# Second layer's compression MLP half a gate later, a fixed order of preparation, and A's attention in one group for each row tile

## The chip, the cores and the metric

One core of one Trainium2 chip runs the whole program. The metric is device time in microseconds (us), the median of several executions; one execution was taken with the hardware profiler, and its trace is what the rows below are from. Engines: PE is TensorE's matmul side, DVE is VectorE, ACT is ScalarE, POOL is GpSimd, SP is SyncE, whose queue issues the DMAs.

## The reference

Two layers of a decoder trunk on x of 256 tokens by 1024. In each layer h = RMSNorm(x), and one projection h @ w_in feeds four token mixers and four merge gates:

```
A  sparse attention: an indexer scores all keys, the best 64 of each query are attended to
   (4 query heads, one shared key/value head that comes from a latent of 128)
B  block attention, causal over all 256 keys (4 heads)
C  NSA: compressed blocks of 32 tokens (an MLP: gelu(z @ w1) @ w2), selected blocks, a window
D  sliding window of 128 with sinks (2 key/value heads)
br    = mixer output (256 wide) @ w_branch[n]             for each of the four
x     = x + (sum over n of sigmoid(gate[n]) * br[n]) @ w_out
x     = x + ConvFFN(RMSNorm(x))                           up, depthwise conv, SiLU product, down
```

Queries and keys of each mixer are normed per head and rotated first. That is the mixer's preparation.

## The kernel before

The program is written by a planner. Every piece of work is a Python generator that yields the engine, the values it needs and the buffer rings it takes from; `Flow.run` keeps a clock for each engine, always lets on the generator that can start earliest (then by priority), and so fixes the order of each engine's instructions when the program is built. On the chip each engine then runs its own list in order and waits where data are late.

Weights come in chunks of up to 1 MB in the order of the list `plan`, through a ring of three `raw` buffers on SP's queue. Each chunk is split in pieces of 128 x 1024 into a high part (`hi`, on ACT) and a low part (`lo`, on DVE), four buffers each. A product takes three matmuls: high by high, high by the low part of the activations, low by high. A raw buffer comes free when its last `lo` is done. An exception is the first weight of the compression MLP (`hidden`), which is used as it lands: its raw buffer comes free when its matmuls are done.

The generator `main` writes the large matmuls in a fixed order. First the projection columns, mixer by mixer in the order A, C, B, D. Then comes the list `SEQ`: gates in halves of 512 columns, the two MLP products for the keys and values of C (`hidden`, 64 matmuls on 32-row tiles in all), and the branch products. Mixer work goes in between wherever the planner finds it ready. TensorE's list is one queue: what stands behind a `hidden` that waits, waits too.

A mixer's preparation works in one shared set of buffers (`prep_r`, a ring of one): a mixer takes it, squares and sums its heads, takes a reciprocal root on POOL, rotates, transposes, and gives it back. The order in which the four get it is whatever the planner comes to. Preparation of C ends in the MLP's input `z` (the sums `kr<-kn,col`), for which `hidden` waits.

The attention of a mixer is `attend2`: scores of both row tiles (128 queries each) in one visit, for which two banks of the ring `mm_r` and both of `sc_r` are taken, then a softmax for each tile, then the value products of both tiles in one visit (`values`). Scores run on 64-row tiles of the array, value products on 64-column tiles, everything else on the whole array. A's `attend2` needs the selection masks of both tiles, `sel[0]` and `sel[1]`, which DVE finds in eight rounds of maximum and replace for each tile.

In the trace all instructions of a helper carry line L214, so tile names tell them apart: `mm<-hi,ahi` is a gate or projection product, `mm<-raw,kr` the MLP, `tr<-cst,f` a transpose, `mm<-qk` and `sc<-qk` scores, `tr<-f,kvA` A's value products.

Of the kernel before, what the change touches and what calls it, by code (L numbers as in the profile page):

```python
# [12 lines left out]
ALU = mybir.AluOpType  # L13
# [218 lines left out]
def trunk(ctx: ExitStack, tc: tile.TileContext, a, out):  # L232
# [151 lines left out]
    def rows_chunk(src, k0, k1, c0, c1):  # L384
# [7 lines left out]
        if not plan:  # L392
# [1 line left out]
        plan.append(Chunk(ap, (nk, n), cut))  # L394


    SEQ = [("gate", 0, 0), ("gate", 0, 1), ("hidden", 0, 0), ("hidden", 1, 0), ("gate", 1, 0),
           ("gate", 1, 1), ("branch", 0, 0), ("branch", 0, 1), ("gate", 2, 0), ("gate", 2, 1),
           ("branch", 1, 0), ("branch", 1, 1), ("gate", 3, 0), ("branch", 2, 0), ("branch", 2, 1),
           ("branch", 3, 0), ("gate", 3, 1), ("branch", 3, 1)]  # L400
    FIRST, LAST = [n for op, n, _ in SEQ if op == "branch"][0], SEQ[-1][1]
    PRIO = (4, 19, 7, 6)
    PORDER = (0, 2, 1, 3)
    CH_A, CH_C = [(0, 384), (384, 680)], [(1448, 1832), (1832, 2100)]
# [4 lines left out]
    for l in range(DEPTH):  # L409
        wi = a["w_in"][l]  # L410
        for kg in range(2):
            for _, c0, c1 in COLS[:2]:
                rows_chunk(wi, 4 * kg, 4 * kg + 4, c0, c1)
        for _, c0, c1 in COLS[2:]:
            for kg in range(2):
                rows_chunk(wi, 4 * kg, 4 * kg + 4, c0, c1)
        for op, n, half in SEQ:
            if op == "gate":
                for kg in range(2):
                    c0 = 2612 + n * D + half * 512  # L420
                    rows_chunk(wi, 4 * kg, 4 * kg + 4, c0, c0 + 512)
            elif op == "hidden":
                ap = a["c_cmp_w1"][l, n].rearrange("(c p) h -> p c h", p=128)
                plan.append(Chunk(ap, (16, 128), []))
            elif n == LAST:
                rows_chunk(a["w_branch"][l, n], 0, 2, half * 512, half * 512 + 512)
            elif half == 0:
                ap = a["w_branch"][l, n].rearrange("(k p) n -> p k n", p=128)
                plan.append(Chunk(ap, (2, D), [lambda v, h=h: v[:, :, h * 512:h * 512 + 512] for h in range(2)]))
        for kg in range(2):  # L430
            for half in range(2):
                rows_chunk(a["w_out"][l], 4 * kg, 4 * kg + 4, half * 512, half * 512 + 512)
        up = a["w_up"][l].rearrange("(k p) (g n) -> p k g n", p=128, g=2)
        for c in range(0, KF, 2):
            for g in range(2):
                plan.append(Chunk(up[:, :, g, c * 128:c * 128 + 256], (8, 256),
                                  [lambda v, h=h: v[:, :, h * 128:h * 128 + 128] for h in range(2)]))
        for half in range(2):
            for k0, k1 in DOWN:
                rows_chunk(a["w_down"][l], k0, k1, half * 512, half * 512 + 512)  # L440
# [188 lines left out]
    def T_pairs(o, src, n, needs):  # L629
# [8 lines left out]
        tr_r.give(tb, te)  # L638
        return te

    def attend2(prio, qT, kblk, kT, vfn, scl, masks, y, needs, sink=None, fin=None, gates=None):

        got = yield "PE", needs, [sx_r, sm_r, sx_r, sm_r, mm_r, mm_r, sc_r, sc_r]
        P.side = 2
        for t in range(NT):
            nk = 128 * (t + 1)

            for hh in range(2):
                for par in range(2):
                    b = 64 * par  # L650
                    te = P.matmul(got[4 + 2 * t + par][:, hh * nk:hh * nk + nk], qT[b:b + 64, hh, t * 128:t * 128 + 128],
                                  kT[b:b + 64, kblk(2 * hh + par), :nk], start=True, stop=True)
        P.side = 1
        pts, evs = [None, None], [[Fut() for _ in range(t + 1)] for t in range(NT)]
        for t in range(NT):
            fl.spawn(softmax(t, got[2 * t], got[2 * t + 1], got[4 + 2 * t:6 + 2 * t], (mm_r, sc_r)[t], te, scl, masks[t], sink,
                             None if gates is None else gates[t], pts, evs[t]), prio + t)
        yield from values(vfn, pts, evs, y, gates is not None, fin)
# [140 lines left out]

    def dsa(l, pa, pf, y, yf):  # L800
        m = M[l]
        (prep,) = yield "ACT", [pf, col_f[l]], [prep_r]
        rt, qr, kr, kn = prep
        latT = kn[:, :, 128:256]
        tl = yield from head_rstd(pa[:, :, None, 256:384], 1, 128, sm1["rl"], rt, [])
# [34 lines left out]
        for t in range(NT):  # L840
# [12 lines left out]
        tq = yield from T_pairs(qT, qr, 2, [tq])  # L853
        tk = yield from T_pairs(kT, krd, 1, [tk])
        prep_r.give(prep, tk)
        fin = qk_done(qk, [], yf, 1)
        fl.spawn(attend2(10, qT, lambda h: 0, kT, lambda h, b: kvA[:, b, 64:128], th(sm1["sA"], H), sel,
                        y, [tq, tk] + self_f, fin=fin), 10)

    def indexer(t, iqT, ikT, iw, needs, fin, f):  # L860
        nk = 128 * (t + 1)
# [32 lines left out]
        f.t = V.tensor_tensor(sel[t], sel[t], mask, op=ALU.min)  # L894

    def moba(l, pb, pf, y, yf):
        (prep,) = yield "ACT", [pf, tab_f[l]], [prep_r]
        rt, qr, kr, kn = prep
        tr = yield from head_rstd(heads(pb[:, :, 0:512]), 8, DH, sm1["rB"], rt, [])
        yield from scaled(sm1["sB"], sm1["rB"], 8, tr)  # L900
        tq = yield from rope(qr.rearrange("p t (h u d) -> p t h u d", u=1, d=64), heads(pb[:, :, 0:256]), H, DH,
                             cc[:, 2], ss_[:, 2], rt, [])
        (qk,) = yield "PE", [], [qk_r]
        qT, kT = qk[:, 0:512].rearrange("p (k s) -> p k s", k=2), qk[:, 512:1024].rearrange("p (k s) -> p k s", k=2)
        tq = yield from T_pairs(qT, qr, 2, [tq])
        yield "DVE", [], []
        tn = V.tensor_tensor(heads(kn), heads(pb[:, :, 256:512]),
                        th(sm1["rB"], 8)[:, :, 4:8, None].to_broadcast([128, NT, H, DH]), op=ALU.mult)
        tk = yield from rope(kr.rearrange("p t (h u d) -> p t h u d", u=1, d=64), heads(kn), H, DH, cc[:, 3], ss_[:, 3], rt, [tn])
        tk = yield from T_pairs(kT, kr, 2, [tk])  # L910
        prep_r.give(prep, tk)
        fin = qk_done(qk, [], yf, 1)
        fl.spawn(attend2(20, qT, lambda h: h // 2, kT, lambda h, b: pb[:, b, 512 + 64 * h:576 + 64 * h],
                        th(sm1["sB"], H), [tri[:, 128:], tri], y, [tq, tk], fin=fin), 20)

    def swa(l, pd, pf, y, yf):
        (prep,) = yield "ACT", [pf, tab_f[l]], [prep_r]
        rt, qr, kr, kn = prep
        tr = yield from head_rstd(heads(pd[:, :, 0:384]), 6, DH, sm1["rD"], rt, [])
        yield from scaled(sm1["sD"], sm1["rD"], 6, tr)  # L920
        tq = yield from rope(qr.rearrange("p t (h u d) -> p t h u d", u=1, d=64), heads(pd[:, :, 0:256]), H, DH,
                             cc[:, 8], ss_[:, 8], rt, [])
        (qk,) = yield "PE", [], [qk_r]
        qT, kT = qk[:, 0:512].rearrange("p (k s) -> p k s", k=2), qk[:, 512:1024].rearrange("p (k s) -> p k s", k=2)
        tq = yield from T_pairs(qT, qr, 2, [tq])
        yield "DVE", [], []
        knv = heads(kn[:, :, 0:128])
        tn = V.tensor_tensor(knv, heads(pd[:, :, 256:384]),
                        th(sm1["rD"], 6)[:, :, 4:6, None].to_broadcast([128, NT, 2, DH]), op=ALU.mult)
        tk = yield from rope(kr.rearrange("p t (h u d) -> p t h u d", h=2, d=64), knv, 2, DH, cc[:, 9], ss_[:, 9], rt, [tn], dup=2)  # L930
        tk = yield from T_pairs(kT, kr, 2, [tk])
        prep_r.give(prep, tk)
        fin = qk_done(qk, [], yf, 1)
        fl.spawn(attend2(30, qT, lambda h: h // 2, kT,
                        lambda h, b: pd[:, b, 384 + 64 * (h // 2):448 + 64 * (h // 2)], th(sm1["sD"], H),
                        [tri[:, 128:], dmask], y, [tq, tk], sink=M[l]["sink"], fin=fin), 30)

    def nsa(l, pc, pf, y, yf, hid):
        m = M[l]
        (prep,) = yield "DVE", [pf, tab_f[l]], [prep_r]  # L940
        rt, qr, kr, kn = prep
        kvd = kr.rearrange("p t (i u d) -> p t i u d", i=2, u=2)
        t1 = yield from rope(kvd[:, :, 0:1], pc[:, :, None, 256:320], 1, DH, cosd, sind, rt, [], dup=2)
# [322 lines left out]
    def main():  # L1266
# [13 lines left out]
        for l in range(DEPTH):  # L1280
# [11 lines left out]
            proj = (pa, pb, pc, pd)  # L1292
            ys = [p[:, :, 0:256] for p in proj]
            yf = [Fut() for _ in range(4)]
            def mixer(n, f):
                if n == 2:
                    fl.spawn(nsa(l, pc, f, ys[2], yf[2], hid), PRIO[2])
                else:
                    fl.spawn((dsa, moba, None, swa)[n](l, proj[n], f, ys[n], yf[n]), PRIO[n])
# [65 lines left out]
                        k0 = 4 * half + 2 * j  # L1365
                        fl.spawn(rows_T(mg[:, :, 128 * k0:128 * k0 + 256], [f], mT, k0, mf[2 * half + j], scale=0.5), 2)

            order = [n for op, n, half in SEQ if op == "branch" and half == 0]
            for i, n in enumerate(order):
                yTs[n] = [], Fut()  # L1370
                fl.spawn(y_T(ys[n], yf[n], *yTs[n]), 2)
            for op, n, half in SEQ:
                if op == "gate":
                    yield from gate_of(n, half)
                elif op == "hidden":
                    yield from hidden(n, next(it), hid)
                else:
                    yield from branch_out(n, half)
# [108 lines left out]
```

## Time and profile before

| | |
|---|---|
| median of 3 runs | 851.69 us (851.65 to 853.23) |
| the profiled execution | 850.18 us, span 848.4 us |
| PE busy | 835.4 us, 98% of the span |
| DVE, ACT, POOL busy | 673.0, 543.8, 36.5 us |
| mean granted TensorE clock | 0.994 |
| DMA | 149.91 MB, mean 177 GB/s |

The span is from the first to the last instruction. A busy PE is not PE at its peak: matmuls are pipelined and their ends are modelled, so the step from one start to the next tells more than a duration.

### The profile page before, as it was taken

The page shows a single profiled execution, that of the slowest core. Times are in us where ns is not written, and L with a number is a line of the kernel's source. Part 1 is how long each engine was busy: PE and PEld are TensorE (multiplying, and loading weights), DVE is VectorE, ACT ScalarE, POOL GpSimd, SP SyncE. Part 2 cuts the span into 40 slices and gives each one's busy share as a digit, 9 for nine tenths or more (in the row PEclk, how much of TensorE's full clock was granted, in tenths as well). Part 3 has the DMA queues.
Part 4 walks back from the last instruction along what each step waited for, and adds up shares of the span by engine and source line. Part 5 has one row for each costly group of instructions (what it writes and reads, how often), then busy time and mean ns, then how long its engine had stood idle before and what let it go on. Part 6 is the DMA issues. An engine that isn't in the chain of part 4 may idle for free.

```text
span 848.4 us, 14190 instructions
## 1 busy us (share of the span) xinstructions
PE 835.4 (98%) x5459; PEld 733.1 (86%) x5459; DVE 673.0 (79%) x1327; ACT 543.8 (64%) x941; POOL 36.5 (4%) x33
## 2 busy tenths in 40 slices
PE   9999999999999999999999997999999999999998
PEld 8987787888899999978898875878878999999886
DVE  5799989788579999975458989977676799999552
ACT  6673775765478888844366667766445788888431
POOL 0111111000000000000001110100000000000000
PEclk9999999999999999999999997999999999999999
DMA  7754563444647666546456453435455465665550
GB/s 264 248 199 149 178 216 106 159 162 153 219 138 229 207 201 197 186 153 210 132 168 211 157 173 115 148 117 182 162 192 192 149 199 199 200 199 199 175 197 26
DMA packets 103414, 149.91 MB, mean 177 GB/s; under 512 B 4072, under 2 KB 62258, under 8 KB 103346
## 3 DMA queue, kind: packets, MB, share of 16 engines
q1 hardware_dynamic: 103346, 149.00, 52.6%
q8 instruction: 43, 0.70, 0.3%
q14 instruction: 25, 0.20, 0.1%
HBM read 147.94 MB, written 1.05 MB: 176 GB/s over the span
## 4 chain that ended last, share of the span: by engine, by line
PE 86%; DVE 7%; DMA 2%; POOL 2%; ACT 1%; issue 1%; SPq 0%; DVEq 0%; ACTq 0%
PE mm L214 75%; PE tr L214 6%; PE sc L214 5%; DVE lo L214 2%; DMA raw<-in_w_in_dram 1%; POOL rB L214 1%; DVE acc L214 1%; DVE rt L214 1%; DMA x<-in_x_dram 1%; POOL rD L214 1%; DVE m L214 1%; DVE f L214 1%; ACT f L214 0%; ACT hi L214 0%; SPq L242 0%
## 5 line engine op out<-in xcount | busy, mean ns | idle before, releaser
L214 DVE TENSOR_TENSOR lo<-raw,hi 128x1024 fp32r<-128x1024 f32 (+2 forms) x280 | 328.7, 1179 | 99.4 <-ACT hi L214 95.3
L214 ACT ACTIVATE hi<-raw 128x1024 fp32r<-128x1024 f32 (+2 forms) x280 | 283.0, 1022 | 152.6 <-PE mm L214 132.4
L214 PE MATMUL mm<-hi,ahi 128*128 128x512 f32 (+4 forms) x480 | 176.0, 372 | 0.6 <-ACT hi L214 0.6
L214 PE MATMUL mm<-hi,alo 128*128 128x512 f32 (+4 forms) x480 | 172.2, 364 | 0.0
L214 PE MATMUL mm<-ahi,hi 128*128 128x256 f32 x640 | 149.9, 276 | 0.0
L214 PE MATMUL mm<-alo,hi 128*128 128x256 f32 x640 | 149.7, 276 | 0.0
L214 PEld LDWEIGHTS mm<-alo,hi 128*128 128x128 f32 x640 | 120.1, 188 | 0.1
L214 PEld LDWEIGHTS mm<-ahi,hi 128*128 128x128 f32 x640 | 120.2, 188 | 0.1
L214 PE MATMUL mm<-lo,ahi 128*128 128x512 f32 (+4 forms) x480 | 118.2, 369 | 0.0
L214 PEld LDWEIGHTS mm<-hi,ahi 128*128 128x128 f32 x480 | 90.2, 188 | 15.2 <-issue 1.7
L214 PEld LDWEIGHTS mm<-hi,alo 128*128 128x128 f32 x480 | 90.3, 188 | 12.0
L214 PEld LDWEIGHTS mm<-lo,ahi 128*128 128x128 f32 x480 | 83.0, 188 | 13.2 <-issue 1.3
L214 PE MATMUL mm<-hi,slotQ 128*128 128x512 f32 x352 | 89.6, 395 | 0.0
L214 PE MATMUL mm<-ahi,lo 128*128 128x256 f32 x640 | 86.9, 276 | 0.0
L214 PEld LDWEIGHTS mm<-hi,slotQ 128*128 128x128 f32 x352 | 66.1, 188 | 15.4
L214 PEld LDWEIGHTS mm<-ahi,lo 128*128 128x128 f32 x640 | 79.1, 188 | 0.0
L214 ACT ACTIVATE f<-f,col 128x256 f32<-128x256 f32 x88 | 48.1, 594 | 6.4 <-DVE f L214 6.4
L214 PE MATMUL mm<-lo,slotQ 128*128 128x512 f32 x176 | 48.7, 396 | 0.0
L214 PEld LDWEIGHTS mm<-lo,slotQ 128*128 128x128 f32 x176 | 33.0, 188 | 7.6
L214 ACT ACTIVATE qk<-f,col 128x256 f32<-128x256 f32 x88 | 39.2, 495 | 0.0
L214 ACT ACTIVATE f<-f,nmx 128x128 f32<-128x128 f32 (+1 forms) x80 | 35.3, 444 | 4.7 <-DVE nmx L214 4.7
L214 DVE SCALAR_TENSOR_TENSOR f<-f,col,f 128x254 f32<-128x254 f32 x88 | 38.2, 478 | 0.0
(235 smaller groups left out, 1038.6 us busy)
## 6 DMA issues: line engine op xcount, KB each, us to landing
raw<-in_w_up_dram SPq DMA_DIRECT2D x44, 1024.0 KB, 5.0
raw<-in_w_in_dram SPq DMA_DIRECT2D x40, 1024.0 KB, 4.8
raw<-in_w_down_dram SPq DMA_DIRECT2D x20, 1024.0 KB, 4.9
raw<-in_w_out_dram SPq DMA_DIRECT2D x8, 1024.0 KB, 5.3
raw<-in_w_branch_dram SPq DMA_DIRECT2D x6, 1024.0 KB
raw<-in_w_in_dram SPq DMA_DIRECT2D x7, 768.0 KB
raw<-in_w_in_dram SPq DMA_DIRECT2D x4, 592.0 KB, 3.7
raw<-in_w_in_dram SPq DMA_DIRECT2D x4, 536.0 KB, 5.7
```

The costliest lines, as they stand in the source:

```text
L214: fn(*a, **k)
```

## The change

Three things change. `SEQ` becomes one list for each layer, and in the second layer's the two `hidden` stand behind the first half of gate 1 instead of ahead of it; the order of weight loads follows. A table `order_of` fixes the order in which the mixers take the preparation buffers (A, B, C, D in the first layer, A, B, D, C in the second), with a future for each turn, and C asks for them as a step of ACT instead of DVE. And mixer A uses a new generator `attend`, once for each row tile, instead of `attend2`: each takes only the two `sc_r` banks, waits for its own tile's mask, and writes its own half of the output.

```diff
-    SEQ = [("gate", 0, 0), ("gate", 0, 1), ("hidden", 0, 0), ("hidden", 1, 0), ("gate", 1, 0),
+    SEQS = [[("gate", 0, 0), ("gate", 0, 1), ("hidden", 0, 0), ("hidden", 1, 0), ("gate", 1, 0),
            ("gate", 1, 1), ("branch", 0, 0), ("branch", 0, 1), ("gate", 2, 0), ("gate", 2, 1),
...
+            [("gate", 0, 0), ("gate", 0, 1), ("gate", 1, 0), ("hidden", 0, 0), ("hidden", 1, 0),
+           ("gate", 1, 1), ("branch", 0, 0), ("branch", 0, 1), ("gate", 2, 0), ("gate", 2, 1),
...
-        for op, n, half in SEQ:
+        for op, n, half in SEQS[l]:
...
+    def attend(t, qT, kblk, kT, vfn, scl, mask, y, needs, sink=None, fin=None, gate=None):
+        nk = 128 * (t + 1)
...
+        sxt, sm, *scs = yield "PE", needs, [sx_r, sm_r, sc_r, sc_r]
...
+        P.side = 2
+        for hh in range(2):
+            for par in range(2):
+                b = 64 * par
+                te = P.matmul(scs[par][:, hh * nk:hh * nk + nk], qT[b:b + 64, hh, t * 128:t * 128 + 128],
+                              kT[b:b + 64, kblk(2 * hh + par), :nk], start=True, stop=True)
+        P.side = 1
+        for par in range(2):
+            fl.spawn(attend_max(t, scs[par], te, par, Sx, nk, mask, scl, sink, mx, tx, sc_r), 8)
...
+        ob, = yield "PE", tes, [tr_r]
+        op = ob[:, :256].rearrange("p (k q) -> p k q", k=2)
+        P.side = 2
+        for k in range(2):
+            for b in range(t + 1):
+                for par in range(2):
+                    te = P.matmul(op[64 * par:64 * par + 64, k, :], vfn(2 * k + par, b), pT[:, 2 * k + par, b, :],
+                                  start=b == 0, stop=b == t)
+        P.side = 1
+        pt_r.give(pTt, te)
+        yt = y[:, :, t * 128:t * 128 + 128]
+        if gate is None:
+            eng, _ = yield "AV", [te], []
+            te = copy_on(eng, yt, op)
...
     def dsa(l, pa, pf, y, yf):
         m = M[l]
-        (prep,) = yield "ACT", [pf, col_f[l]], [prep_r]
+        (prep,) = yield "ACT", [pf[0], pf[1], col_f[l]], [prep_r]
+        pf[2]()
...
-        fin = qk_done(qk, [], yf, 1)
-        fl.spawn(attend2(10, qT, lambda h: 0, kT, lambda h, b: kvA[:, b, 64:128], th(sm1["sA"], H), sel,
-                        y, [tq, tk] + self_f, fin=fin), 10)
+        fin = qk_done(qk, [], yf, NT)
+        for t in range(NT):
+            fl.spawn(attend(t, qT, lambda h: 0, kT, lambda h, b: kvA[:, b, 64:128], th(sm1["sA"], H), sel[t],
+                            y, [tq, tk, self_f[t]], fin=fin), 10 + t)
...
     def nsa(l, pc, pf, y, yf, hid):
         m = M[l]
-        (prep,) = yield "DVE", [pf, tab_f[l]], [prep_r]
+        (prep,) = yield "ACT", [pf[0], pf[1], tab_f[l]], [prep_r]
+        pf[2]()
...
+            order_of = ((0, 1, 2, 3), (0, 1, 3, 2))[l]
+            turn = dict((n, Fut()) for n in order_of)
+            turn[order_of[0]].t = 0.0
+
+            def next_turn(n):
+                i = order_of.index(n) + 1
+                if i < 4:
+                    turn[order_of[i]].t = 0.0
+
             def mixer(n, f):
+                f = [f, turn[n], lambda: next_turn(n)]
```

## Rows read from the trace of the kernel before

**Rows 1.** The page's part 1: busy us, share of the span, instructions.

```profile
PE 835.4 (98%) x5459; PEld 733.1 (86%) x5459; DVE 673.0 (79%) x1327; ACT 543.8 (64%) x941; POOL 36.5 (4%) x33
```

**Rows 2.** Waits of PE, nine rows: us in total, times, longest us.

```profile
PE tr L214 <- DVE kr L214: 3.0, 1, 3.0
...
PE tr L214 <- DVE qr L214: 0.6, 1, 0.6
...
PE tr L214 <- ACT f L214: 0.2, 1, 0.2
```

**Rows 3.** PE's timeline, second layer: start, us, operation, [idle before <-releaser].

```profile
514.05 1.18 PE L214 MATMUL mm<-lo,ahi 128*128 128x512 f32 x4
518.21 1.09 PE L214 MATMUL tr<-cst,kr 128*128 128x128 f32 x4 [2.98 <-DVE kr L214]
521.10 1.09 PE L214 MATMUL tr<-cst,kr 128*128 128x128 f32 x4 [1.80 <-DVE den L214]
521.98 1.06 PE L214 MATMUL tr<-cst,f 128*128 128x128 f32 x4
524.06 3.55 PE L214 MATMUL mm<-raw,kr 128*15 128x128 f32 x64 [1.02 <-DVE kr L214]
...
528.39 0.48 PE L214 MATMUL mm<-hi,ahi 128*128 128x512 f32 x1
...
614.57 0.39 PE L214 MATMUL sc<-hi,yhi 128*128 128x512 f32 x1
```

**Rows 4.** Stretches of 2 us: PE, PEld, DVE, ACT, POOL busy; PEclk, DMA.

```profile
518.00:520.00 2.00, 1.09 (x4) 0.72 (x4) 1.54 (x8) 1.22 (x7) 0.00 (x0) 0.50 0.60 234
...
528.00:530.00 2.00, 2.00 (x14) 1.77 (x13) 2.00 (x3) 1.08 (x2) 0.00 (x0) 1.00 1.02 378
```

**Rows 5.** PE's timeline, first layer.

```profile
82.35 0.40 PE L214 MATMUL mm<-hi,alo 128*128 128x512 f32 x1
82.67 0.71 PE L214 MATMUL mm<-qk 64*128 64x128 f32 x8
...
98.97 0.50 PE L214 MATMUL mm<-hi,ahi 128*128 128x512 f32 x1
99.31 0.39 PE L214 MATMUL mm<-hi,alo 128*128 128x512 f32 x1
99.54 0.39 PE L214 MATMUL mm<-hi,ahi 128*128 128x512 f32 x1
...
101.92 1.94 PE L214 MATMUL mm<-raw,kr 128*15 128x128 f32 x64
```

**Rows 6.** DVE's timeline, first and second layer.

```profile
94.34 1.18 DVE L214 TENSOR_TENSOR kr<-kn,col 128x120 f32<-128x120 f32 x4
...
513.82 1.22 DVE L214 TENSOR_TENSOR lo<-raw,hi 128x1024 fp32r<-128x1024 f32 x1
...
523.65 1.16 DVE L214 TENSOR_TENSOR kr<-kn,col 128x120 f32<-128x120 f32 x4
...
592.80 0.68 DVE L214 TENSOR_TENSOR slotQ<-slotQ,tr 128x512 f32<-128x512 f32 x1
```

**Rows 7.** POOL's timeline: the mixers' reciprocal roots.

```profile
98.12 2.54 POOL L214 TENSOR_TENSOR rC<-rC,mhalf 128x8 f32<-128x8 f32 x1 [21.65 <-DVE rC L214]
...
131.20 3.17 POOL L214 TENSOR_TENSOR rD<-rD,mhalf 128x12 f32<-128x12 f32 x1 [9.22 <-DVE rD L214]
...
506.77 2.31 POOL L214 TENSOR_TENSOR rD<-rD,mhalf 128x12 f32<-128x12 f32 x1 [18.28 <-DVE rD L214]
525.68 1.64 POOL L214 TENSOR_TENSOR rC<-rC,mhalf 128x8 f32<-128x8 f32 x1 [16.61 <-DVE rd L214]
```

**Rows 8.** The chain that ended last, a piece of gate matmuls: start, us, what.

```profile
208.26 12.97 PE mm L214 x56
```

**Rows 9.** SP's timeline: a weight load is issued.

```profile
515.07 0.37 SPq L242 DMA_DIRECT2D raw<-in_w_in_dram  x1
```

**Rows 10.** DMA issues from 440 to 570: KB each, median us to landing.

```profile
raw<-in_w_in_dram SPq DMA_DIRECT2D x15, 1024.0 KB, 4.8
```

More of the change, by code (lines that the diff above doesn't have):

```diff
@@ L394, in rows_chunk @@
         plan.append(Chunk(ap, (nk, n), cut))
-    SEQ = [("gate", 0, 0), ("gate", 0, 1), ("hidden", 0, 0), ("hidden", 1, 0), ("gate", 1, 0),
+    SEQS = [[("gate", 0, 0), ("gate", 0, 1), ("hidden", 0, 0), ("hidden", 1, 0), ("gate", 1, 0),
            ("gate", 1, 1), ("branch", 0, 0), ("branch", 0, 1), ("gate", 2, 0), ("gate", 2, 1),
            ("branch", 1, 0), ("branch", 1, 1), ("gate", 3, 0), ("branch", 2, 0), ("branch", 2, 1),
-           ("branch", 3, 0), ("gate", 3, 1), ("branch", 3, 1)]
-    FIRST, LAST = [n for op, n, _ in SEQ if op == "branch"][0], SEQ[-1][1]
+           ("branch", 3, 0), ("gate", 3, 1), ("branch", 3, 1)],
+            [("gate", 0, 0), ("gate", 0, 1), ("gate", 1, 0), ("hidden", 0, 0), ("hidden", 1, 0),
+           ("gate", 1, 1), ("branch", 0, 0), ("branch", 0, 1), ("gate", 2, 0), ("gate", 2, 1),
+           ("branch", 1, 0), ("branch", 1, 1), ("gate", 3, 0), ("branch", 2, 0), ("branch", 2, 1),
+           ("branch", 3, 0), ("gate", 3, 1), ("branch", 3, 1)]]
+    FIRST, LAST = [n for op, n, _ in SEQS[0] if op == "branch"][0], SEQS[0][-1][1]
     PRIO = (4, 19, 7, 6)
@@ L639, in T_pairs @@
         return te
+    def attend(t, qT, kblk, kT, vfn, scl, mask, y, needs, sink=None, fin=None, gate=None):
+        nk = 128 * (t + 1)
+        rdf = Fut()
+        tx = []
+        sxt, sm, *scs = yield "PE", needs, [sx_r, sm_r, sc_r, sc_r]
+        Sx = sxt.rearrange("p (h n) -> p h n", h=H)
+        mx, nmx, den, es, rd = (sm[k] for k in ("mx", "nmx", "den", "es", "rd"))
+        P.side = 2
[7 more added lines that the diff above has]
+            fl.spawn(attend_max(t, scs[par], te, par, Sx, nk, mask, scl, sink, mx, tx, sc_r), 8)
+        yield "DVE", [_Pair(tx)], []
+        tm = V.tensor_scalar(nmx, mx, -1.0, None, op0=ALU.mult)
+        for h in range(H):
+            yield "ACT", [tm], []
+            te = A.activation(Sx[:, h, :nk], Sx[:, h, :nk], AF.Exp, bias=nmx[:, h:h + 1], accum_out=den[:, h:h + 1])
+        if sink is not None:
+            yield "DVE", [tm], []
+            t2 = V.tensor_tensor(es, sink, nmx, op=ALU.add)
+            yield "ACT", [t2], []
+            t2 = A.activation(es, es, AF.Exp)
+            yield "DVE", [t2, te], []
+            t2 = V.tensor_tensor(den, den, es, op=ALU.add)
+        else:
+            t2 = te
+        fl.spawn(recip(t2, den, rd, gate, rdf), 8)
+        tn = []
+        for h in range(H):
+            eng, _ = yield "AV", [rdf], []
+            if eng == "ACT":
+                tn.append(A.activation(Sx[:, h, :nk], Sx[:, h, :nk], AF.Copy, scale=rd[:, h:h + 1]))
+            else:
+                tn.append(V.tensor_scalar(Sx[:, h, :nk], Sx[:, h, :nk], rd[:, h:h + 1], None, op0=ALU.mult))
+        tes = []
+        pTt = None
+        for g in range(t + 1):
+            if g == 0:
+                pTt, tb = yield "PE", tn if t == 0 else tn[:2], [pt_r, tr_r]
+                pT = pTt.rearrange("p (h b q) -> p h b q", h=H, b=2)
+            else:
+                tb, = yield "PE", tn[2:], [tr_r]
+            if t == 0:
+                tp = tb.rearrange("p (h q) -> p h q", h=H)
+                for h in range(H):
+                    tq = P.transpose(tp[:, h, :], Sx[:, h, :128], ident)
+                dst = pT[:, :, 0, :]
+            else:
+                tp = tb.rearrange("p (h b q) -> p h b q", h=2, b=2)
+                for hh in range(2):
+                    for b in range(2):
+                        tq = P.transpose(tp[:, hh, b, :], Sx[:, 2 * g + hh, b * 128:b * 128 + 128], ident)
+                dst = pT[:, 2 * g:2 * g + 2]
+            f = Fut()
+            tes.append(f)
+            fl.spawn(evac_tr(dst, tp, tb, tq, f), 9)
+        sx_r.give(sxt, tq)
+        sm_r.give(sm, max(tn))
+        ob, = yield "PE", tes, [tr_r]
[12 more added lines that the diff above has]
+            te = copy_on(eng, yt, op)
+        else:
+            yield "DVE", [te], []
+            te = V.tensor_tensor(yt, yt, op, op=ALU.add)
+        tr_r.give(ob, te)
+        fin(te)
@@ L896, in moba @@
     def moba(l, pb, pf, y, yf):
-        (prep,) = yield "ACT", [pf, tab_f[l]], [prep_r]
+        (prep,) = yield "ACT", [pf[0], pf[1], tab_f[l]], [prep_r]
+        pf[2]()
         rt, qr, kr, kn = prep
@@ L916, in swa @@
     def swa(l, pd, pf, y, yf):
-        (prep,) = yield "ACT", [pf, tab_f[l]], [prep_r]
+        (prep,) = yield "ACT", [pf[0], pf[1], tab_f[l]], [prep_r]
+        pf[2]()
         rt, qr, kr, kn = prep
@@ L939, in nsa @@
         m = M[l]
-        (prep,) = yield "DVE", [pf, tab_f[l]], [prep_r]
+        (prep,) = yield "ACT", [pf[0], pf[1], tab_f[l]], [prep_r]
+        pf[2]()
         rt, qr, kr, kn = prep
@@ L1366, in branch_out @@
                         fl.spawn(rows_T(mg[:, :, 128 * k0:128 * k0 + 256], [f], mT, k0, mf[2 * half + j], scale=0.5), 2)
-            order = [n for op, n, half in SEQ if op == "branch" and half == 0]
+            order = [n for op, n, half in SEQS[l] if op == "branch" and half == 0]
             for i, n in enumerate(order):
@@ L1371, in main @@
                 fl.spawn(y_T(ys[n], yf[n], *yTs[n]), 2)
-            for op, n, half in SEQ:
+            for op, n, half in SEQS[l]:
                 if op == "gate":
```

## The prediction

> **What bounds the kernel now.** I read the page's first part, then the waits of TensorE, then TensorE's own timeline where those waits lie, and last VectorE and the DMA queue in that stretch. The page says that TensorE is busy for 835.4 us, 98% of the span of 848.4 [rows 1]. The reader should take from it that the kernel is bound by matmul work, that nothing taken off another engine counts by itself, and that what can be won is what TensorE loses. The view of waits lists that loss: nine rows, 8.8 us in sum, the longest a single wait of 3.0 us for VectorE [rows 2].
>
> The timeline says where it is [rows 3]. The second layer's gate 0 ends with the matmuls of 514.05 (end 515.23). Gate 1 does not follow; the compression MLP does, as the written order has it. Its input comes from the NSA mixer, the last of the layer to be prepared, and VectorE is still at work on it. So TensorE idles for 2.98, 1.80 and 1.02 us (5.80 in all) around a dozen transposes, and gate 1 begins at 528.39, 13.2 us after gate 0's end. The granted clock falls on the way: 0.50 in the stretch from 518 to 520, 1.00 again from 528 [rows 4]; those are the 1.2 and the 2.4 GHz level. At the low level the MLP's 64 matmuls take 3.55 us, in the first layer, at the full one, 1.94 [rows 3, 5].
>
> VectorE puts the last term of the MLP's input down at 523.65 plus 1.16, so 524.8 [rows 6]. In the first layer it does so at 95.5, and the MLP begins at 101.92 [rows 5, 6]: 6.4 us to spare, no wait.
>
> **The fixed order of preparation.** The reciprocal roots on GpSimd give the order that is there already: in the first layer mixer C's root at 98.12 is ahead of D's at 131.20, in the second D's at 506.77 is ahead of C's at 525.68 [rows 7]; A and B come before both. The new table asks for A, B, C, D and A, B, D, C. No instruction is added, and none changes its place on that account: 0 us. That C now asks for ScalarE rather than VectorE at its start only shifts the moment at which the planner lets it in, after the buffers of the mixer before are given back, which is what it waited for anyway. I bound it by 0 and by the 0.6 us of the wait for `qr` [rows 2], and take 0.
>
> **The MLP half a gate later.** TensorE gets half of gate 1 at 515.2 instead of the wait. One half gate is 8 row groups by 2 row tiles by 3 products, 48 matmuls; the chain of waits has 56 in 12.97 us, 0.232 each [rows 8], so 11.1 us. Their weights: two of the four pieces are split before the gap (the second ends at 513.82 + 1.22 [rows 6]), and the other chunk now loads ahead of the MLP's two, so it is there long before.
>
> What is won: the wait of 5.80; the low clock on the MLP, 3.55 - 1.94 = 1.61; and the low clock on twelve transposes. Four of them take 1.09 us in the first row and 0.85 to the next issue in a pair of rows (521.10 to 521.98: 0.88, 0.22 each) [rows 3]; at twice the clock 0.11 each, so 12 x 0.11 = 1.3. Sum 8.7 us. Checked from the other side: 13.2 us lie between the gates, the work in them at full clock is some 20 transposes at 0.11 and 1.9 of MLP, 4.1 us, and 9.1 remain. I take 8.7.
>
> Does half a gate cover it? TensorE is done with it at 515.2 + 11.1 + twelve transposes and their entries, 1.6, so 527.9. VectorE must split the two later pieces in front of the MLP's input, 2 x 1.22 us, which moves 524.8 to 527.2. So it does, by 0.7 us, and half of that again comes back because VectorE waits less for transposes at the low clock. The margin is thin. If VectorE is 2 us later than this, TensorE waits some 1.3 us, and about half as much again if the clock falls as it does here (1.61 + 1.3 on 5.80).
>
> The moved loads: the queue waits for one of three raw buffers at each chunk. The MLP's two chunks now hold theirs from behind gate 1's first half, so that the second half's first chunk goes out when the fourth piece is split, near 523, and lands 4.8 us later [rows 10], 528. It needs 1 us more to be split, and TensorE wants it when the MLP is done, near 530. Queued behind it are the second half's other chunk and the first branch weights, which need the MLP's buffers: out near 530, landed near 535, wanted after another 5.5 us of matmuls plus the interleaved mixer work. Cost 0, at most 1 to 2 us if the split comes late. Today the same queue entry goes out at 515.07 [rows 9], and nothing waits for it.
>
> Mixer C ends later by the shift of the MLP, about 3 us: its last sum of `y` stands at 592.80 plus 0.68 [rows 6], so 596.5. TensorE, 8 us ahead by then, asks for it at 606 instead of 614.57, where branch 2 begins [rows 3]. No wait is due.
>
> **Separate groups for A's two tiles.** Products, transposes and elementwise work are the same in number. Added: the scores and the value products each go in two visits to the packed 64-row or 64-column form instead of one, that is 2 visits a layer, 4 in all. A visit costs at its entry 82.35 to 82.67, 0.32 instead of 0.23 us, and at its exit 98.97 to 99.31, 0.34 instead of 0.23 [rows 5]: 0.20 a visit, 0.8 us in all, on the bounding engine. The lower bound is 0 (a tile's group may stand directly behind another packed group). The upper adds a wait at the head of each, as for `qr`, 0.6 [rows 2]: 3.2 us. I take 0.8, as waits at such heads are rare in the list. The page TensorEngine Tiling (Array Packing) of the Trainium skill, section Tiling Modes, says that a change of tiling mode drains the array, which speaks against this part of the change. The steps of 0.32 and 0.34 agree with it; by the rule alone, with the whole modelled overlap of 0.16 us (0.39 less 0.23) lost at both ends of four visits, the term would be 1.3 instead of 0.8, and the sum below 0.5 us smaller.
>
> What the split frees is worth nothing on the path: no row of the waits is for a branch's operands, two PSUM banks of the gates' ring come free but no gate waits for one. The output copy in two halves is VectorE's or ScalarE's, outside the bound.
>
> **Sum.** -8.7 + 0.8 + 0.2 for the transposes' entries into the gate's stream = -7.7 us. The profiled execution took 850.18 us (span 848.4 and 1.8 around it), so 842.5 there; the median of the runs is 851.69, and 844.0 is what I forecast for it.
>
> **The rivals.** *Cover too short.* VectorE has the input 2 to 4 us later than worked out, because the split pieces and A's earlier softmax push in front of it. For: VectorE has hardly a pause in this stretch, 0.7 us of margin. Against: A's work is the same in sum and goes earlier. It gives back 2 to 4 us and part of the clock: 846 to 849.
>
> *The next weights are late.* As above, one chunk lands late after the MLP: 1 to 2 us, 845.5.
>
> *Slower: waits at the heads of the new groups.* TensorE runs its queue in order, and the planner places A's groups by its own costs. Scores of the first tile now stand in the queue while VectorE sorts the second tile; if the chip is behind the plan, every matmul behind them waits. Price: 0.6 (`qr`) to 3.0 us (`kr`) [rows 2] at each of four added visits. It decides from 7.7 / 4 = 1.9 us a visit; at 3.0 it would be 844 + 12 = 856. Against: in the whole trace only one wait reaches that, and it is the planned one.
>
> *Given back later.* C's `y` 10 us later than I have it, and branch 2 waits as the MLP does now: about 851.5.
>
> **Chances and range.** Wait gone, 842.5 to 845.5: 0.58. Cover too short: 0.15. Late weights: 0.05. Given back: 0.08. Slower by heads: 0.14. The point is the likeliest case's 844.0, whose own range is 842.5 to 845.5; the stated range goes from 842.3 to 851.5, which leaves out the slower rival and a few hundredths below. 0.2%, about 1.7 us, is what a measurement of this kernel can tell from no change. Faster: the first three cases, 0.78. Within it: most of the fourth, 0.08. Slower: 0.14.
>
> **What would show it.** In the profile after, the second layer's gate 0 is followed by 24 or more gate matmuls with transposes between, then the 64 MLP matmuls in about 1.9 us; the clock is 1.00 throughout 510 to 535; the waits of TensorE sum to about 3 us instead of 8.8. The forecast is wrong if an idle of over 1 us stands in front of the MLP or of the gate half behind it, if A's score or value groups show waits before them, or if the first layer's MLP, which has 6.4 us to spare, comes to wait too.

## The result and the profile after

The changed kernel took 841.95 us (median of 4 runs, 841.23 to 842.79), the kernel before beside it 851.67 (4 runs, 849.28 to 853.23). The ratio is 0.9889 [0.9864, 0.9914]: faster by 1.1%, 9.7 us. In five later rounds it was 840.97 against 851.3, ratio 0.9877 [0.9864, 0.9891]. Sign and mechanism are those of the forecast; the time lies 2 us below its point of 844.0, and 0.35 below the lower end of its range.

The profiled execution took 841.81 us, its span is 840.0 where that of before was 848.4. The page's first part, of which TensorE's figures are to be held against [rows 1]:

```profile
PE 833.5 (99%) x5459; PEld 731.7 (87%) x5459; DVE 671.6 (80%) x1316; ACT 546.6 (65%) x954; POOL 35.8 (4%) x33
```

The waits of TensorE, complete, where [rows 2] had nine with 8.8 us in sum (columns: us in total, times, longest):

```profile
PE sc L214 <- DVE f L214: 1.0, 1, 1.0
PE mm L214 <- ACT hi L214: 0.7, 1, 0.7
PE sc L214 <- DMA rn<-in_norm_g_dram: 0.4, 1, 0.4
PE tr L214 <- DVE qr L214: 0.2, 1, 0.2
PE sc L214 <- DVE slotP L214: 0.2, 1, 0.2
```

The sum is 2.5 us now, 6.3 less, and busy time is 1.9 us less: 8.2 of the 8.4 by which the span fell. What replaced the gap of [rows 3] stands in TensorE's timeline of the second layer (start, us, operation; no row has an idle time in front of it):

```profile
515.78 0.39 PE L214 MATMUL mm<-hi,ahi 128*128 128x512 f32 x1
...
518.52 0.60 PE L214 MATMUL tr<-cst,kr 128*128 128x128 f32 x4
...
522.16 0.60 PE L214 MATMUL tr<-cst,kr 128*128 128x128 f32 x4
...
525.44 1.53 PE L214 MATMUL tr<-f,slotQ 128*64 128x128 f32 x24
526.90 0.72 PE L214 MATMUL mm<-qk 64*128 64x128 f32 x8
527.45 1.03 PE L214 MATMUL sc<-qk 64*128 64x256 f32 x8
528.41 1.20 PE L214 MATMUL mm<-lo,ahi 128*128 128x512 f32 x4
...
532.29 1.94 PE L214 MATMUL mm<-raw,kr 128*15 128x128 f32 x64
534.16 0.50 PE L214 MATMUL mm<-hi,ahi 128*128 128x512 f32 x1
...
606.07 0.40 PE L214 MATMUL sc<-hi,yhi 128*128 128x512 f32 x1
```

Between 515.78 and 532.29 the reader sees the first half of gate 1 with the transposes in it, which used to stand alone in an idle queue. The MLP takes 1.94 us for its 64 matmuls, as in the first layer [rows 5], and not 3.55 [rows 3]. The clock agrees, in the windows that answer to [rows 4]:

```profile
518.00:520.00 2.00, 2.00 (x15) 1.74 (x14) 0.86 (x4) 2.00 (x8) 0.00 (x0) 1.00 0.96 268
...
528.00:530.00 2.00, 2.00 (x13) 1.41 (x10) 1.99 (x7) 2.00 (x3) 0.00 (x0) 1.00 0.00 0
```

It is granted in full, 2.4 GHz, through the whole stretch; in the kernel before the window from 518 to 520 was at 0.50, 1.2 GHz. Last, VectorE's timeline, against [rows 6]:

```profile
521.37 1.22 DVE L214 TENSOR_TENSOR lo<-raw,hi 128x1024 fp32r<-128x1024 f32 x1
...
524.22 1.17 DVE L214 TENSOR_TENSOR kr<-kn,col 128x120 f32<-128x120 f32 x4
...
602.38 0.69 DVE L214 TENSOR_TENSOR slotQ<-slotQ,tr 128x512 f32<-128x512 f32 x1 [1.01 <-PE tr L214]
603.77 0.69 DVE L214 TENSOR_TENSOR ylo<-slotQ,yhi 128x512 fp32r<-128x512 f32 x1 [0.70 <-ACT yhi L214]
```

The MLP's input is complete at 524.22 + 1.17 = 525.39, 6.9 us before the MLP. But mixer C's last sum of `y` has moved from 593.5 to 603.1, and TensorE begins branch 2 at 606.07 instead of 614.57. Of 21 us between the sum and the branch three are left, and making the operand's two halves (to 604.46) takes half of these.

By stages, cut at VectorE's residual sums: the second layer's mixer stage took 231.84 us before and takes 223.87, which is -7.97; all that lies ahead of it gives -0.41, and what comes behind it is the same to 0.01. The two parts are not equally sure: the kernel before reaches the start of this stage between 423.4 and 424.5 us in its six profiles (the one of the prediction and five further ones, below), the changed kernel at 424.1 and 423.5 in its two, so the 0.41 lies within the scatter of one kernel, and 8 us do not.

### The profile page after: what moved, and what is told of

Same layout as the page of the kernel before. It is cut to its first block, busy times and chain, and to the rows that moved or that the text cites. A ratio compares the mean times of both kernels' runs of the same rounds, so it can differ in the third digit from the quotient of the medians.

```text
span 840.0 us, 14179 instructions
## 1 busy us (share of the span) xinstructions
PE 833.5 (99%) x5459; PEld 731.7 (87%) x5459; DVE 671.6 (80%) x1316; ACT 546.6 (65%) x954; POOL 35.8 (4%) x33
## 4 chain that ended last, share of the span: by engine, by line
PE 92%; DVE 4%; DMA 2%; issue 1%; ACT 1%; POOL 0%; SPq 0%; DVEq 0%; ACTq 0%
PE mm L214 81%; PE tr L214 6%; PE sc L214 5%; DMA raw<-in_w_in_dram 1%; DVE lo L214 1%; DVE acc L214 1%; POOL rB L214 0%; DMA rn<-in_norm_g_dram 0%; DVE m L214 0%; ACT hi L214 0%; DVE f L214 0%; SPq L242 0%; DVE slotP L214 0%; DVE rB L214 0%; ACT slotP L214 0%
```

## The experiments

**How much one execution can tell.** Both kernels again, in five rounds.

> The kernel before, unchanged, for the spread of its executions. Theory (the wait costs a different amount in each execution, because the granted clock comes back at different moments): its executions spread over 3 to 4 us around 851.5, and the slower ones have the lower mean clock, about 0.99 against 0.994 and more in the faster ones; 0.001 of clock is about 0.85 us. Rival (the spread comes from the start, the loads or the measurement): the spread is as wide, but clock and time do not go together.

> The changed kernel, unchanged, for the size of the gain over five rounds. Theory: executions between 841 and 843, clocks 0.997 to 1.000, a gain of 9 to 10 us on the median, of which 8.4 is the trace's and 1.5 the low clock that the profiled execution of before happened to be spared. Rival (the profiled execution was typical): the gain over five rounds is 8.0 to 8.6.

The copy of the kernel before came to 850.54 against 851.3 (ratio 0.9996 [0.9987, 1.0005]), with runs from 849.6 to 852.75. The copy of the changed kernel had 840.86 to 841.25, a spread of 0.4. So the kernel before scatters by 3 us and the changed one, in this group, hardly at all. The median gain is 10.3 us, above both the theory's 9 to 10 and the rival's 8.0 to 8.6; between the two profiled executions it is 8.7 (849.71 and 841.02). The second layer's mixer stage took 231.82 and 223.72.

Clock and time go together in part. Of 66 executions of the kernel before, those of the later rounds and of the single profiles below, 18 have a mean granted clock of 0.996 and a median of 850.1 us, 48 have 0.994 and 851.3; within each of the two the times still lie 2 to 3 us apart.

**The move alone.** Before with the second layer's list changed, nothing else (`SEQ` becomes one list for each layer, as in the change; shown is the line that differs in the second):

```diff
-            [("gate", 0, 0), ("gate", 0, 1), ("hidden", 0, 0), ("hidden", 1, 0), ("gate", 1, 0),
+            [("gate", 0, 0), ("gate", 0, 1), ("gate", 1, 0), ("hidden", 0, 0), ("hidden", 1, 0),
...
```

> Only the second layer's MLP is put half a gate later; mixer A keeps one group for both tiles, no order table. By the prediction's ledger: the wait of 5.8 us and the low clock go, 8.7 less 0.2, so 8.5 less in the trace and some 10 on the median, and the first layer stays as it was with its wait of 0.65 for qr. Rival (the gain needs A's split, which frees VectorE earlier): a rest of the wait stays in front of the MLP, gain 4 to 6.

It took 842.05 (841.49 to 842.27), ratio 0.9889 [0.9874, 0.9904]; the stage 223.72, -8.12. The gain in this stage is the move's, and the rival, that it needs A's split, is out. TensorE's timeline at the two places where it can fail:

```profile
527.49 1.07 PE L214 MATMUL mm<-raw,kr 128*15 128x128 f32 x32
...
606.02 0.50 PE L214 MATMUL mm<-hi,yhi 128*128 128x512 f32 x1 [0.32 <-ACT yhi L214]
606.75 0.50 PE L214 MATMUL mm<-hi,ylo 128*128 128x512 f32 x1 [0.22 <-DVE ylo L214]
```

The MLP begins at 527.49 with no wait, its input being complete at 525.17, so half a gate covers by 2.3 us. Behind it, branch 2 waits 0.32 and 0.22 us for mixer C's `y`: the half gate uses up what there was to spare at that end.

**The separate groups alone.** The changed kernel with the old list in both layers, without the table, and with C asking for VectorE again:

```diff
-            [("gate", 0, 0), ("gate", 0, 1), ("gate", 1, 0), ("hidden", 0, 0), ("hidden", 1, 0),
+            [("gate", 0, 0), ("gate", 0, 1), ("hidden", 0, 0), ("hidden", 1, 0), ("gate", 1, 0),
...
-        (prep,) = yield "ACT", [pf[0], pf[1], tab_f[l]], [prep_r]
+        (prep,) = yield "DVE", [pf[0], pf[1], tab_f[l]], [prep_r]
...
-                f = [f, turn[n], lambda: next_turn(n)]
+                f = [f, 0.0, lambda: None]
```

> Only mixer A's attention is split in a group for each tile; the MLP stays where it was. By the ledger: plus 0.8 us for four added visits to the packed forms, the wait before the MLP as it was, clock about 0.994: 851 to 853. Rival (the split moves the MLP's input forward): the wait shrinks by 1 to 2 us, 848 to 850. Rival (waits at the heads of new groups): 853 and more, with waits before sc products on qk.

851.84 (850.12 to 852.87), ratio 1.0005 [0.9996, 1.0013]: nothing. The waits are there still, shared out otherwise:

```profile
PE tr L214 <- DVE kr L214: 2.6, 1, 2.6
PE tr L214 <- DVE hsum L214: 1.7, 1, 1.7
PE tr L214 <- DVE qr L214: 1.3, 3, 0.6
...
PE mm L214 <- DVE kr L214: 0.4, 1, 0.4
```

The mean granted clock of the profiled execution is 0.997 instead of 0.994, and that wins nothing either.

Counted in TensorE's timeline as changes from whole-array work to work on part of it (the start-up's and the indexer's small groups included), the packed form is entered 22 times in the kernel before, 26 times here, 21 with the move alone and 24 in the changed kernel. What a visit costs can't be read here: the second layer has 13 instead of 10, and its mixer stage takes 232.43 us, which lies among the 231.8 to 233.7 of the six profiles of the kernel before. It can be read where no wait and no low clock is in the way. Between the move alone and the changed kernel the second layer has two visits more; TensorE's idle time in the stage falls from 0.90 to 0.43 and 0.44 us (two profiles), the stage is 0.15 and 0.00 us longer, so the visits took 0.46 to 0.62, 0.23 to 0.31 each, against the 0.20 that the prediction read from steps [rows 5]. The first layer's one visit more shows no price.

**The same split for a second mixer.** The changed kernel, with B's scores and values in a group for each tile too:

```diff
-        fin = qk_done(qk, [], yf, 1)
-        fl.spawn(attend2(20, qT, lambda h: h // 2, kT, lambda h, b: pb[:, b, 512 + 64 * h:576 + 64 * h],
+        fin = qk_done(qk, [], yf, NT)
+        for t in range(NT):
+            fl.spawn(attend(t, qT, lambda h: h // 2, kT, lambda h, b: pb[:, b, 512 + 64 * h:576 + 64 * h],
...
```

> The changed kernel with mixer B's attention split in a group for each tile too: four more visits to the packed forms. By the ledger 4 x 0.20 = 0.8 us more, 841.8 against 841.0. By the rule that a change of mode drains the array, 1.3 more. Rival (a visit costs nothing here, since groups stand directly behind each other and waits before them shrink, as A's split showed with 0.4 less in the first layer): 840.5 to 841.1.

844.71 (843.75 to 845.03), ratio 0.9925 [0.9912, 0.9938]; 3.7 us more than the changed kernel's 840.97, where 0.8 was expected. The packed form is entered 29 times, 5 more. In the second layer two of them cost 0.56 and 0.71 us against the changed kernel's two profiles, 0.28 to 0.35 each. In the first layer it is 2.3 us for three, and over half of that is no visit's price (TensorE's timeline):

```profile
179.18 0.50 PE L214 MATMUL mm<-hi,ahi 128*128 128x512 f32 x1 [0.55 <-DVE slotP L214]
...
180.72 0.50 PE L214 MATMUL mm<-hi,ahi 128*128 128x512 f32 x1 [0.80 <-DVE slotP L214]
```

Gate products wait twice for VectorE's merge buffer, 1.35 us; the changed kernel has no such wait. The rest is some 0.3 us a visit. What a split moves in another engine's queue can cost more than the visits; which instruction of VectorE's is in the way was not pursued.

**The clock without the wait's cause removed.** Before with 72 filler matmuls (128x256, results unused) in the gap, so that TensorE has work while it waits:

```diff
+    def fill(hid):
+        ps, = yield "PE", [], [mm_r]
...
+        while hid.ready.t is None or fl.clock["PE"] < hid.ready.t:
+            te = P.matmul(ps[:, :S], ahi[:, 0, 0:128], ahi[:, 0, :], start=True, stop=True)
+            yield "PE", [], []
...
+                    if l == 1 and n == 0:
+                        fl.spawn(fill(hid), 1000)
```

> The kernel before with 72 idle-filling matmuls (128 x 256, read by nobody) in front of the second layer's MLP; the wait stays, only TensorE is not idle in it. Theory (the low clock that follows the wait is a price of its own, and larger in the median execution than in the profiled one): the clock stays at 1.00, the MLP takes 1.94 us, and the time falls by 2.3 us (2.9 less 0.6 for more filling than the wait needs) plus the 1 to 1.5 us by which the median lies above the profiled execution: 847 to 848.5, executions within 1.5 us of each other. Rival (the median's excess comes from elsewhere): 849 to 850, and a spread of 3 us as in the kernel before.

849.76 (848.86 to 851.77) against 850.62, ratio 0.9991 [0.9982, 1.0001], which isn't told from no change. Median and spread are the rival's, not the theory's. The clock stays at 1.00, and TensorE's timeline shows what that is worth:

```profile
521.83 0.60 PE L214 MATMUL tr<-cst,kr 128*128 128x128 f32 x4
...
522.74 2.15 PE L214 MATMUL mm<-ahi 128*128 128x256 f32 x16
524.82 1.94 PE L214 MATMUL mm<-raw,kr 128*15 128x128 f32 x64
...
527.53 0.48 PE L214 MATMUL mm<-hi,ahi 128*128 128x512 f32 x1
```

The MLP runs in 1.94 us, but begins at 524.82, later than the 524.06 of before. VectorE's four sums for it are not there sooner (VectorE's timeline):

```profile
523.88 1.19 DVE L214 TENSOR_TENSOR kr<-kn,col 128x120 f32<-128x120 f32 x4
```

They end between 524.25 and 525.08, where before it was 524.01 to 524.80, and the fillers stand in front of the MLP for another 0.5 us behind the first of them. Gate 1 starts at 527.53 instead of 528.39 [rows 3], 0.9 us won; with fillers that end in time it might be 1.4, by an estimate from these rows. The low clock by itself is the smaller part; the transposes that it slowed lay inside the wait for VectorE. The 8.1 us of the move are the loss to that wait, and come back only with other work in it.

**Where the kernel before scatters.** Four more profiles of it, single executions.

> The kernel before once more, for another profile of the wait. Theory: the stretch at the low clock begins and ends elsewhere against the wait than in the first profile; where it ends after the MLP, gate matmuls run at 0.46 instead of 0.23 us a step and the second layer is longer by half of what is left of the stretch. Rival: the stretch ends with the MLP each time, and executions differ in the start alone.

> The same, a third profile. Theory and rival as for the second.

> The kernel before once more, for its profile: where the profiled execution lies among the runs (848 to 850 us of span so far) and how long the granted clock stays low in the second layer. Theory: the executions differ by how long the low clock reaches past the wait, 0 to 2 us into gate 1, and by start-up. Rival: they differ in the other stages, and the low clock's stretch is the same in a long and a short execution.

> As the look before it: span between 847.9 and 850.5 us; by the theory a longer one shows the low clock past 529 us, a shorter one ends it before 528; by the rival there is no such order.

With the first profile and that of the copy in five rounds there are six. The end of the low clock is worked out from the granted clock in windows of 1 and 2 us:

| execution, us | span, us | clock low until, us |
|---|---|---|
| 849.71 | 847.9 | 526.7 |
| 849.86 | 848.0 | 526.9 |
| 850.00 | 848.1 | 527.4 |
| 850.18 (that of the prediction) | 848.4 | 527.4 |
| 850.68 | 848.9 | 528.1 |
| 851.73 | 850.0 | 530.0 |

The order is the same in both columns. Part of that is that the longer executions are later ahead of it already: the MLP itself ends between 527.0 and 528.1. The windows of the longest show what it means (the sixth number behind the length, the counts in brackets left aside, is the granted clock):

```profile
526.00:528.00 2.00, 2.00 (x40) 1.30 (x32) 1.84 (x8) 1.84 (x4) 1.64 (x1) 0.50 0.26 34
528.00:530.00 2.00, 2.00 (x13) 1.95 (x10) 1.97 (x4) 0.67 (x2) 0.00 (x0) 0.51 0.96 345
530.00:532.00 2.00, 2.00 (x11) 1.44 (x9) 1.31 (x5) 0.59 (x1) 0.00 (x0) 1.00 1.02 357
```

And its timeline of TensorE, right behind the MLP:

```profile
528.05 1.97 PE L214 MATMUL tr<-cst,f 128*128 128x128 f32 x8
529.67 0.61 PE L214 MATMUL mm<-hi,ahi 128*128 128x512 f32 x1
```

Here 1.9 us of work behind the MLP still run at 1.2 GHz, and from the end of the MLP to that of gate 1's first half it takes 17.8 us instead of 16.9 to 17.1 in the others. Against the second execution of the table this one is 2.0 us longer: 0.9 at this place, the other 1.1 in small pieces ahead of the MLP's end. The theory holds for half of the difference. The rival has a part as well: with fillers, at full clock, the runs still went from 848.86 to 851.77. By stages the six profiles differ in two places: the second layer's mixer stage takes 231.82 to 233.73 us, and the start-up with the first layer's mixers 232.7 to 233.8; the first layer's ConvFFN and all that follows the second layer's mixers agree to 0.02 us.

**A whole gate instead of half.** Before with the MLP behind both halves of gate 1 (the second layer's list alone is shown):

```diff
-            [("gate", 0, 0), ("gate", 0, 1), ("hidden", 0, 0), ("hidden", 1, 0), ("gate", 1, 0),
-           ("gate", 1, 1), ("branch", 0, 0), ...
+            [("gate", 0, 0), ("gate", 0, 1), ("gate", 1, 0), ("gate", 1, 1), ("hidden", 0, 0), ("hidden", 1, 0),
+           ("branch", 0, 0), ...
```

> The kernel before with the second layer's compression MLP a whole gate later (behind both halves of gate 1) instead of half a gate, A unsplit. Theory: the cover of half a gate is already enough (in the run with the MLP alone moved, its input was there 2.3 us early), so nothing more is won in front of the MLP; but mixer C's y came at the very moment that branch 2 asked for it there (waits of 0.32 and 0.22 us), so 11 us more of delay for the MLP must come out as a wait in front of branch 2, less what C makes up: some 5 to 9 us, 847 to 851 us, and the stage from the second layer's mixers to its end near 230 us instead of 223.7. Rival: C's end hangs on VectorE's queue and not on the MLP, no wait appears, 842 us as with half a gate.

852.06 (850.11 to 853.92), ratio 1.0013 [1.0003, 1.0022]: the whole gain is gone. The second layer's mixer stage is 10.3 us longer than with half a gate. TensorE's timeline in front of branch 2:

```profile
605.99 1.24 PE L214 MATMUL tr<-cst,f 128*128 128x128 f32 x4 [3.88 <-DVE f L214]
608.52 1.97 PE L214 MATMUL tr<-cst,f 128*128 128x128 f32 x8 [1.30 <-ACT f L214]
...
614.57 0.50 PE L214 MATMUL mm<-hi,yhi 128*128 128x512 f32 x1 [1.52 <-ACT yhi L214]
615.29 0.51 PE L214 MATMUL mm<-hi,ylo 128*128 128x512 f32 x1 [0.22 <-DVE ylo L214]
```

The waits sum to 6.9 us, for C's softmax and then for its `y`, and again the clock falls behind them:

```profile
604.00:608.00 4.00, 1.24 (x4) 0.69 (x4) 2.31 (x11) 3.88 (x17) 0.00 (x0) 0.73 0.00 1
608.00:612.00 4.00, 3.48 (x24) 3.15 (x26) 0.52 (x2) 2.04 (x4) 0.00 (x0) 0.50 0.00 0
```

So the prediction's fourth rival, that the wait is given back at branch 2, is a real edge of this schedule, one half gate away. The theory's 847 to 851 was a little low. The waits are 6.4 us more than the 0.5 in front of branch 2 with half a gate; TensorE's busy time in the stage is 4.0 us longer, and the low clock, which the theory left out, is the one thing seen that can lengthen it.

**Half a gate in the first layer too.** The changed kernel with the second layer's list in both.

> The changed kernel with the MLP half a gate later in the first layer too. Theory: the first layer's MLP has its input 6.4 us early and loses nothing there, so the move wins nothing: 841 us, unless C's y in the first layer comes too late for its branch, as it nearly does in the second (margin 2.9 us in the changed kernel), which would add 0.5 to 3 us. Rival: the half gate in between also gives TensorE room for other waits of the first layer, such as the one for qr, and the kernel gains 0.5 us or more.

862.16 (859.53 to 864.2), ratio 1.014 [1.0121, 1.0159]: 21 us slower than the changed kernel, against 0 to 3 expected. The second layer keeps its form; its mixer stage is as long as in the changed kernel to 0.2 us. All of it is lost in the first, 17.5 us in the profiled execution, as TensorE's timeline has it:

```profile
114.39 1.94 PE L214 MATMUL mm<-raw,kr 128*15 128x128 f32 x64
...
186.69 1.24 PE L214 MATMUL tr<-cst,f 128*128 128x128 f32 x4 [2.45 <-DVE f L214]
...
196.91 0.50 PE L214 MATMUL mm<-hi,yhi 128*128 128x512 f32 x1 [1.84 <-ACT yhi L214]
...
208.38 1.97 PE L214 MATMUL tr<-cst,f 128*128 128x128 f32 x8 [4.69 <-ACT f L214]
```

The MLP, with its input long there, stands 12.9 us later than in the changed kernel, and the two mixers that are finished last deliver their operands 18 and 19 us later. TensorE waits for both, 11.9 us in all in this layer. Why they come 5 to 6 us later than the MLP's shift was not pursued. The move that won 8 us where the MLP waited costs twice that where it did not.

## Why the prediction came out as it did

**What bounds the kernel** and **the mechanism** held. The loss was the gap of [rows 3], the move alone takes it away, and the clock and the MLP's 1.94 us are as foreseen.

**The fixed order of preparation** at 0: in the program as it is built, the queues of TensorE, GpSimd and SyncE hold the same instructions in the same order with the table and C's request of ScalarE as with neither; one step goes from ScalarE to VectorE, and a few of VectorE's neighbours are exchanged. It was not timed by itself.

**The move**, -8.7 and +0.2 for the transposes' entries, -8.5: the move alone measured -8.12 in the stage, 0.4 short. The terms are not separate causes, though. With the fillers the clock alone is worth 0.9, perhaps 1.4, not 2.9; the sum was nearly right because all of it goes when the wait goes: the transposes' 1.3 us lay inside the wait. (The 0.85 in the prediction's reading of them stands in no row of its pair, which gives the 0.88 that it used.)

**The separate groups**, +0.8 for four visits at 0.20: neither price nor count came out so. In the kernel with the split alone there are four more than before; in the changed kernel two more, three more than with the move alone, as the planner lets a packed group stand right behind another (525.44, 526.90 and 527.45 above are one visit). Two of the three cost 0.23 to 0.31 us each, the third nothing that shows. And the wait for `qr` in the first layer [rows 2], 0.4 to 0.65 us in the six profiles of before and in that of the move alone, is in neither profile of the changed kernel (the 0.2 for `qr` in the list above stands in the second layer); no term had that. In the two profiles that the prediction and the result rest on, the split comes to -0.41 in the first layer and +0.15 in the second, about -0.3 instead of +0.8. The start-up is in the 0.41; counted from 42 us on, behind it, to the layer's residual sum, the changed kernel takes 190.7 us twice, the move alone 191.2, the kernel before 191.0 to 191.4, so that some 0.5 us are the split's with the table. The medians of the same five rounds differ by more, 1.1 us (842.05 and 840.97), and where the rest of that lies isn't known.

On the rule of the Trainium skill, TensorEngine Tiling (Array Packing), section Tiling Modes, that a change of tiling mode drains the array: the 0.23 to 0.35 us a visit measured here agree with it, and lie around the 0.33 (1.3 for four) that the prediction worked out by the rule alone. The visit without a price does not.

**The step that failed** is the one from the trace to the median, with the groups' term as the smaller part. The prediction's sum gave 842.5 for a profiled execution, which took 841.81: 0.7 off, as the groups' term came out 1.1 lower and the move won 0.4 less. To that it added the 1.5 us by which the median of before lay above its own profiled execution, as if any version of the kernel carried them. The changed kernel does not: its median is 0.14 above its profile, in the five rounds 0.05 below it (840.97 and 841.02). 0.7 and 1.4 make the 2.05 us between 844.0 and 841.95.

Which execution of before had been profiled was chance, and 850.18 was a short one: the 66 further executions have a median of 851.2. A good half of the 1.5 stood in the very stage that the change takes the wait from: the second layer's mixer stage was 231.84 us in that execution, and is 0.8 longer in the mean of the five others (231.82 to 233.73); in the changed kernel it is 223.87 and 223.72, and has no such scatter. One piece of it is the tail of the low clock, which ended inside the MLP in the profiled execution and costs others up to 0.9 us more behind it. The changed kernel has next to none of it: its mean clock is 0.999 or 1.000 in seven of eight executions, and 0.997 in the longest, of 842.79 us. Where the rest of the 1.5 stood is not settled; the scatter that remains with the fillers is not the clock's.

**The cover** was said to be 0.7 us, and is 2.3 with the move alone and 6.9 in the changed kernel. VectorE has the input at 525.4, not 527.2. That is not because it waits less for transposes, as the prediction had it: these waits are 1.10 and 0.21 us in this stretch, where before they were 0.46 twice. In the changed kernel the row maxima of B's scores, the last of which stood at 518.18 before, are done by 511.4, and so make room for the split pieces; with the move alone they are not, but only one piece (518.37) is split in front of the input. And TensorE is at the MLP at 532.3, not 527.9, as B's values and D's scores (525.44 to 528.41) stand in the half gate too, 3.0 of the 4.4 us. The two rivals at this place, cover too short and late weights, didn't occur: there is no wait for the MLP's input, and the one for `hi` in the list above stands at 29.25, in the first layer's projections.

**The shift of mixer C** was said to be 3 us, with `y` at 596.5. The MLP moved by 8.2 and the last sum of `y` by 9.6, to 603.1. The forecast held since 21 us lay between sum and branch, but the kernel with the whole gate shows that the step was close to deciding the case: another half gate and the result is no change.

**Waits at the heads of the new groups**, the slower rival, show in no row of the changed kernel.

## What to carry to other kernels

A step that waits for a slow mixer has two edges: in front its own input, behind it what is made from its result; read the time to spare at both before you move it, and move it by no more than the wait needs. The gain of a move is the wait that it covers, in the very stage where that wait stands: the same edit in the layer without the wait cost 17 us and more.

When you turn a trace's difference into a forecast for the median, ask whether the median's excess over the profiled execution belongs to the very wait that you remove. One profiled execution is one draw: of a kernel that scatters by 3 us, two or three more profiles show by stage what repeats and what doesn't.

## What the hardware showed unexpectedly

The low clock's place is not tied to the work. In six executions of one kernel it fell to 0.50 as early as 516.6 us and as late as 519.9, and came back to 1.00 between 526.7 and 530.0, while the MLP, during which or after which it returned, began between 523.4 and 524.5. In the latest case eight transposes behind the MLP took 1.97 us, with the fillers at full clock 1.09. The wait's own length differed by 0.2 us at most (3.0 to 3.2), so a wait of one size leaves a tail of different length. The windows in which it fell, of the earliest and of the latest case, show it in the same sixth number:

```profile
516.00:517.00 1.00, 0.00 (x0) 0.00 (x0) 1.00 (x5) 0.00 (x0) 0.00 (x0) 0.81 0.91 256
...
519.00:520.00 1.00, 0.00 (x0) 0.00 (x0) 0.96 (x5) 1.00 (x7) 0.00 (x0) 0.94 0.12 43
```

In both TensorE did nothing in the window. In the latest case it had done the wait's first four transposes before the fall, at full clock, 0.63 us from 517.86 on; in the earliest they came behind the fall, at 517.70, and took 1.09.
